# A two-layer encoder kernel: triangular inverses in halves of 16, conditioning tiles moved to the delta stage, a copy less in the attention norm, another order of the last rows

## The chip, the cores and the metric

The kernel runs on one core of one Trainium2 chip. The metric is device time in microseconds (us). The engines are PE (TensorE, matrix products; PEld is its weight load), DVE (VectorE), ACT (ScalarE), POOL (GpSimd) and SP (SyncE, which here only issues transfers). Each has a queue of its own that it works off in order; semaphores join them.

## The reference: what is computed

A (512, 1024) fp32 input passes two layers. Each has a token mixer (differential attention, pooling, a short convolution and a gated delta rule, four branches that are gated, summed and projected by `w_o`) and a channel mixer (a dense SwiGLU in layer 0, a top-2-of-8 mixture of experts in layer 1). Norms stand before and after each, and a conditioning vector `c` gives six scale, shift and gate vectors per layer through the weights `ada_w`. The parts that matter here:

```
oa = rms_norm(oa, diff_subln) * (1 - lambda_init)          # attention norm, per head
t_inv = triangular_solve(eye + m, eye, lower=True)         # m strictly lower, chunks of 64
u = t_inv @ (v * beta);  w = t_inv @ (k_beta * exp(g))
v_new = u_n - w_n @ state                                  # scan over chunks
o = qg_n @ state + attn_n @ v_new
state = state * exp(gl_n) + k_d.T @ v_new
```

## The kernel before, in words

An fp32 value is split into a high and a low part, and a product is three matmuls (lines 329 to 331, helper `mm3`). A weight chunk lands in one of three buffers named `raw`; ACT makes the high part (line 295), DVE the low part `wL` (line 296).

A layer's mixer first runs attention, then the delta rule: `delta_mats` (decay matrices, and the inverses), four `delta_group`s (two chunks each, a chain of small products and DVE steps), `delta_out`, and then the `w_o` stage with its norm. A *filler* (`set_fill`, `fill`) hands out PE work that depends on none of this (the merge projections `g_merge`, 128x512 products with weights `w_gb`), a few matmuls at a call, so that PE has work while a chain waits. A scheduler fixes the order on each engine when the program is built.

The inverse: 32 heads-by-chunk units are held as 32x32 diagonal blocks on four groups of 32 partitions. Line 740 negates the block into `Tb`, and the loop of lines 743 to 750 eliminates row after row: 30 steps of one multiply (746) and one subtract (748) on DVE, each up to 240 elements per partition, with a `fill` at every second step. Two transposes follow (752 into `Fi`, 753 into `F`), then copies of `F` and `Fi` into `KQ` (756 on ACT, 757 on DVE). `delta_group` begins with 32x32 products of `F` and `Fi` (793), and goes on through 801 (reads `KQ`), 833 (products with the state `S`), 835 (`vn`, DVE), 840 and 841 (outputs) and 846 (next state).

Conditioning: `g_ada` yields eight tiles for a vector. Each is a 512 KB load into a `raw` buffer (337, issued by SP) and a DVE reduction of 1.22 us (338). Vector (0,2) is a filler beside the merges from the start (`ADA_AT` 0); (0,4) and (0,3) are a filler of the `w_o` stage (argument `late` of `mixer`). In that stage line 380 sums squares with a product, 382 reads the sum on DVE, 384 takes the power on POOL and 390 spreads the factor with a product.

The attention norm (lines 1186 to 1204) does the like: 1191 sums, 1194 reads, 1196 takes the power into `ar`, 1199 copies `ar` over 64 columns into `bt` on DVE, 1201 multiplies `bt` with the identity (four 128x128 products, which the profile shows as eight), 1204 uses the result.

The end: `finish` adds the last expert's rows, norms them and scatters them to the output (2183 to 2194, an indirect transfer by POOL). Behind it stand two loops on a device value that is zero for this input, so that neither body is run: the first stores the last expert (`store`) and sums rows, the second handles windows (2317 and 2320).

Of the kernel before, what the change touches and what calls it, by code (L numbers as in the profile page):

```python
# [17 lines left out]
P = 128  # L18
T = 512
# [3 lines left out]
F = 2816  # L23
# [31 lines left out]
for _name, _w in [("c", KT), ("ada_b", NL * 6 * KT), ("mix_pre", NL * KT), ("mix_post", NL * KT),  # L55
# [16 lines left out]
FILL_ORD = "pbkzqsv"  # L72
ADA_AT = 0
ADA_E = 3
# [12 lines left out]

CST = [("ident", 128), ("ones", 128), ("tri", 128), ("neg", 128), ("edge", 32), ("bd2", 2), ("tok", 4), ("em8", 8),
       ("e8", 8)]
# [5 lines left out]
def shape_constants():  # L95
    c = np.zeros((P, NCST), np.float32), np.zeros((P, NMCST), np.float32)

    def put(name, a):
        late, o, w = C_AT[name]
        c[late][:, o:o + w] = a  # L100
# [18 lines left out]
    put("edge", edge.reshape(P, -1))  # L119
    put("bd2", np.stack([p < 64, p >= 64], 1))  # L120
    put("tok", p[:, None] + P * np.arange(4)[None])
    put("em8", np.tile(np.arange(8)[None] - 8, (P, 1)))
# [112 lines left out]
class Enc:  # L235
# [466 lines left out]
    def delta_mats(self, di):  # L702
# [32 lines left out]

        nc.vector.transpose(L, Sc.rearrange("p u j -> p j u"))
        R = dp.tile([P, 8, 2, 2, 64], FT, name="KQ").rearrange("p c a b t -> p (c a b) t")
        nc.gpsimd.memset(R, 0.0)
        Tb = di.tile([P, 32, 32], FT, name="Tb")
        nc.vector.tensor_scalar(Tb, L, -1.0, None, op0=OP.mult)  # L740
        nc.vector.memset(Tb.rearrange("p a b -> p (a b)")[:, 0:1024:33], 1.0)
        self.delta_prep(0)
        for j in range(1, 31):
            n = 31 - j
            t = di.tile([P, 256], FT, name="Tt", bufs=2)[:, :n * j].rearrange("p (a b) -> p a b", a=n)
            nc.vector.tensor_tensor(t, L[:, j + 1:, j:j + 1].to_broadcast([P, n, j]),
                                    Tb[:, j:j + 1, 0:j].to_broadcast([P, n, j]), op=OP.mult)
            nc.vector.tensor_tensor(Tb[:, j + 1:, 0:j], Tb[:, j + 1:, 0:j], t, op=OP.subtract)
            if j % FILL_T == 0:
                self.fill()  # L750
        dl["Ti"] = F, Fi = [dp.tile([P, 32, 32], FT, name=n) for n in ("F", "Fi")]
        nc.vector.transpose(Fi.rearrange("p u j -> p j u"), Tb)
        nc.vector.transpose(F.rearrange("p u j -> p j u"), Tb.rearrange("p a b -> p b a"))
        for q in range(4):
# [380 lines left out]
    def attention(self, l):  # L1135
# [6 lines left out]
        for pr in range(2):  # L1142
# [54 lines left out]
            pR = self.pt()  # L1197
            rb = self.tmp.tile([P, T], FT, name="bt", bufs=2).rearrange("p (a b c) -> p a b c", a=4, b=2)
            nc.vector.tensor_copy(rb, r.unsqueeze(3).to_broadcast([P, 4, 2, 64]))
            for b in range(4):  # L1200
                nc.tensor.matmul(pR[:, b * P:b * P + P], rb[:, b].rearrange("p a b -> p (a b)"), self.ident,
                                 start=True, stop=True)
            oo = self.tmp.tile([P, T], FT, name="bo", bufs=2)
# [31 lines left out]

    def mixer(self, l, ada, late, to):
        nc, tc = self.nc, self.tc
        self.lay = l
        with ExitStack() as es:
# [50 lines left out]
            self.post_begin(self.scale_col(l, 2, "mix_post", False))  # L1290
            self.set_fill(*[self.g_ada(*x) for x in late])
            for hv in range(2):
# [714 lines left out]

    def store(self, pool, e):

        nc = self.nc  # L2010
        for c, (s0, m, cp) in enumerate(self.blocks(e["cap"])):
            if not isinstance(e["po"][c], list):
                y = self.spare(3)
                nc.scalar.activation(y, e["po"][c], AF.Copy)
                for h in range(2):
                    nc.gpsimd.dma_start(self.yd[e["base"] + s0:e["base"] + s0 + m, h * T:h * T + T], y[64 * h:64 * h + m])
                continue
            for h in range(2):
                o, yh = e["po"][c][h], self.spare((0, 1, 3, 0)[2 * c + h])[:m]
                if cp == 2:  # L2020
                    t = self.bp.tile([P, T], FT, name="bo", bufs=2)
                    nc.scalar.activation(t[:m], o[m:2 * m], AF.Copy)
                    nc.vector.tensor_tensor(yh, o[:m], t[:m], op=OP.add)
                elif h == 0:
                    nc.scalar.activation(yh, o[:m], AF.Copy)
                else:
                    nc.vector.tensor_copy(yh, o[:m])
                nc.gpsimd.dma_start(self.yd[e["base"] + s0:e["base"] + s0 + m, h * T:h * T + T], yh)

# [147 lines left out]
    def finish(self, e):  # L2177

        nc = self.nc
        for c, (s0, m, cp) in enumerate(self.blocks(e["cap"])):  # L2180
            w, x, y = self.sw[:m, c, 1:2], self.sx[c][:m], self.sy[c]
# [7 lines left out]
            R = self.tm_rstd(y, EPS)  # L2189
            for h in range(2):  # L2190
                s = slice(h * T, h * T + T)
                nc.vector.scalar_tensor_tensor(y[h], y[h], R, self.G[:m, s], op0=OP.mult, op1=OP.mult)
                nc.vector.tensor_tensor(x[:, s], x[:, s], y[h], op=OP.add)
            nc.gpsimd.indirect_dma_start(out=self.out, out_offset=bass.IndirectOffsetOnAxis(ap=self.sid[:m, c, 0:1], axis=0),
                                         in_=x, in_offset=None)
# [42 lines left out]
    def moe(self):  # L2238
        nc, tc = self.nc, self.tc
        with ExitStack() as es:  # L2240
# [7 lines left out]
            with tc.tile_pool(name="mps", bufs=1, space=PS) as self.ps:  # L2248
# [66 lines left out]
                self.f = [self.bp.tile([P, T], FT, name=f"f{k}", bufs=1) for k in range(KT)]  # L2315
                n = nc.values_load(ints[0:1, 9 + NW:10 + NW], min_val=0, max_val=1)
                with tc.For_i(0, n):
                    self.store(mw, prev[0])
                    self.sum_rows(mw)
                with tc.For_i(0, n):  # L2320
                    it = mk.tile([P, 1], FT, name="kit")
# [44 lines left out]
    def run(self):  # L2366
# [15 lines left out]
        self.row_of(self.sc, sc)  # L2382
        self.mixer(0, [(0, 2)], [(0, 4), (0, 3)], None)
        self.ffn([(0, 5)] + [(1, v) for v in (1, 0, 2, 4, 3, 5)], self.xd, lambda: (self.scale_col(1, 1, "mix_pre", True), self.mod[1, 0]))
# [7 lines left out]
        nc.vector.tensor_copy(self.tokr, self.C("tok").unsqueeze(2).to_broadcast([P, 4, 2]))  # L2392
        self.mixer(1, [], [], None)
        es_st.close()
# [18 lines left out]
```

## Time and profile before

| | |
|---|---|
| median of three runs | 2619.18 us (2612.95 to 2620.56) |
| the profiled execution | 2621.02 us, of which the span is 2619.2 us |
| mean granted TensorE clock | 0.971 |
| PE busy | 2478.2 us (95%) |
| DVE, ACT, POOL busy | 1599.8 (61%), 1211.8 (46%), 304.1 us (12%) |
| DMA | 478.32 MB, mean 183 GB/s |

The span is the time from the first to the last instruction; the time has 1.8 us more around it. An engine that is busy 95% of the span sets the time, and a change helps where it shortens that engine's work or its idle stretches. A row of a timeline gives the start, the duration, the engine, the line, the operation, output and inputs, shape and count; in brackets stands how long the engine was idle before it, and what released it. A granted clock of 1.00 is 2.4 GHz, one of 0.50 is 1.2 GHz.

### The profile page before, as it was taken

Reading aid. Unit: us, or ns where it says so; the run is one execution under the profiler, and the core shown is the slowest. Engines: PE = TensorE matmul, PEld = TensorE weight load, DVE = VectorE, ACT = ScalarE, POOL = GpSimd, SP = SyncE. Lnnn points to the kernel's source line nnn. Section 1 sums busy time; section 2 is a strip of 40 time slices with the busy share of each in tenths; the row PEclk is TensorE's granted clock in tenths of the full one; section 3 lists DMA queues with packets and bytes.
Section 4 is the critical chain, followed back from the end, with each engine's and each line's share of the span. In section 5 each row is a group of like instructions: output and inputs, shape, how many; then the busy total and the mean of one; then the engine's idle time right before and its main releaser. Section 6 shows DMA issues by size and latency. Waiting matters only on the chain. (4 is left out here: it accounts for less than half of the span.)

```text
span 2619.2 us, 42410 instructions
## 1 busy us (share of the span) xinstructions
PE 2478.2 (95%) x16106; PEld 2012.9 (77%) x16106; DVE 1599.8 (61%) x2914; ACT 1211.8 (46%) x2153; POOL 304.1 (12%) x304
## 2 busy tenths in 40 slices
PE   7999899989999989999899979999999999999996
PEld 6667677889888888677678878886667767899885
DVE  7675833676545566675634556665555557866685
ACT  4554433443333354554333525554444446765574
POOL 0101222240000021103122110000000001000111
PEclk8999999999999999999999979999999999999998
DMA  7123122454565443121222338567889889975681
GB/s 266 57 69 127 61 72 72 152 176 165 179 211 202 144 147 105 49 77 46 77 71 73 111 120 326 210 224 286 309 304 351 324 306 347 383 272 209 239 320 64
DMA packets 124564, 478.32 MB, mean 183 GB/s; under 512 B 14224, under 2 KB 16912, under 8 KB 97600
## 3 DMA queue, kind: packets, MB, share of 16 engines
q1 hardware_dynamic: 119808, 460.19, 49.1%
q0 software_dynamic: 4544, 15.34, 1.7%
q8 instruction: 128, 2.10, 0.3%
q14 instruction: 84, 0.69, 0.1%
HBM read 462.17 MB, written 13.30 MB: 182 GB/s over the span
## 5 line engine op out<-in xcount | busy, mean ns | idle before, releaser
L329 PE MATMUL mm<-hH,wH 128*128 128x512 f32 (+1 forms) x1264 | 490.0, 389 | 9.0 <-ACT hH L1047 4.4
L331 PE MATMUL mm<-hH,wL 128*128 128x512 f32 (+1 forms) x1264 | 480.6, 380 | 5.0 <-DVE wL L296 4.8
L330 PE MATMUL mm<-hL,wH 128*128 128x512 f32 (+1 forms) x1264 | 480.2, 380 | 1.2 <-DVE hL L1282 1.1
L1847 DVE TENSOR_TENSOR mL<-mraw,mH 128x1024 fp32r<-128x1024 f32 x286 | 343.9, 1222 | 176.5 <-ACT mH L1846 121.1
L295 ACT ACTIVATE wH<-raw 128x512 fp32r<-128x512 f32 (+3 forms) x400 | 246.2, 624 | 419.2 <-PE mm L330 305.1
L296 DVE TENSOR_TENSOR wL<-raw,wH 128x512 fp32r<-128x512 f32 (+3 forms) x400 | 280.6, 716 | 214.0 <-ACT wH L295 212.5
L1846 ACT ACTIVATE mH<-mraw 128x1024 fp32r<-128x1024 f32 x286 | 297.6, 1054 | 151.7 <-PE gu L1870 48.5
L1869 PE MATMUL gu<-hH,mH 128*128 128x384 f32 (+1 forms) x1056 | 313.4, 365 | 2.3 <-DVE hL L1805 1.7
L329 PEld LDWEIGHTS mm<-hH,wH 128*128 128x128 f32 x1264 | 241.6, 191 | 63.0 <-issue 7.6
L331 PEld LDWEIGHTS mm<-hH,wL 128*128 128x128 f32 x1264 | 241.4, 191 | 56.3 <-DVE wL L296 8.4
L330 PEld LDWEIGHTS mm<-hL,wH 128*128 128x128 f32 x1264 | 242.4, 192 | 46.8 <-issue 5.9
L1870 PE MATMUL gu<-hH,mL 128*128 128x192 f32 (+1 forms) x1056 | 268.3, 254 | 0.0
L1869 PEld LDWEIGHTS gu<-hH,mH 128*128 128x128 f32 x1056 | 199.0, 188 | 15.1 <-issue 8.5
L1870 PEld LDWEIGHTS gu<-hH,mL 128*128 128x128 f32 x1056 | 202.3, 192 | 0.8
L1869 PE MATMUL gu<-hL,mH 128*128 128x384 f32 (+1 forms) x704 | 195.8, 356 | 0.0
L1847 DVE TENSOR_TENSOR mL<-f,mH 128x512 fp32r<-128x512 f32 x220 | 140.4, 685 | 74.1 <-ACT mH L1846 57.0
L1870 PE MATMUL gu<-hL,mL 128*128 128x192 f32 (+1 forms) x704 | 172.6, 245 | 0.0
L1846 ACT ACTIVATE mH<-f 128x512 fp32r<-128x512 f32 x220 | 126.4, 621 | 63.4 <-PE gu L1870 39.1
L1869 PEld LDWEIGHTS gu<-hL,mH 128*128 128x128 f32 x704 | 132.7, 189 | 9.1 <-issue 4.9
L1870 PEld LDWEIGHTS gu<-hL,mL 128*128 128x128 f32 x704 | 135.3, 192 | 1.5 <-issue 0.8
L338 DVE CUSTOM_DVE_ANT_0 adr<-adr,ada 128x1024 f32<-128x1024 f32 x56 | 68.6, 1224 | 103.3 <-DMA adr<-in_ada_w 103.3
L329 PE MATMUL mm<-mH,ma 128*128 128x512 f32 (+1 forms) x308 | 126.4, 410 | 0.4 <-ACT ma L1887 0.4
(643 smaller groups left out, 4397.6 us busy)
## 6 DMA issues: line engine op xcount, KB each, us to landing
mraw<-in_moe_w SPq DMA_DIRECT2D x209, 1024.0 KB
f<-in_moe_w SPq DMA_DIRECT2D x220, 256.0 KB
raw<-in_w_gb SPq DMA_DIRECT2D x64, 640.0 KB
adr<-in_ada_w SPq DMA_DIRECT2D x56, 512.0 KB
raw<-in_w_in SPq DMA_DIRECT2D x40, 512.0 KB
raw<-in_ada_w SPq DMA_DIRECT2D x32, 512.0 KB
raw<-in_ffn_d SPq DMA_DIRECT2D x58, 256.0 KB
raw<-in_ffn_g SPq DMA_DIRECT2D x24, 512.0 KB
```

The costliest lines, as they stand in the source:

```text
L295: self.nc.scalar.activation(h, part, AF.Copy)
L296: self.nc.vector.tensor_tensor(l, part, h, op=OP.subtract)
L329: t.matmul(out, W[0], X[0], start=start, stop=False)
L330: t.matmul(out, W[0], X[1], start=False, stop=False)
L331: self.last_mm = t.matmul(out, W[1], X[0], start=False, stop=stop).ins
L338: self.nc.vector.tensor_tensor_reduce(r, r, self.sc, 1.0, 0.0, op0=OP.mult, op1=OP.add, accum_out=t[:, m:m + 1])
L1846: self.mark(self.nc.scalar.activation(h[:, s], x, AF.Copy))
L1847: self.mark(self.nc.vector.tensor_tensor(l[:, s], x, h[:, s], op=OP.subtract))
L1869: t.matmul(pp[i][:, f, :2 * n], w[0], X[k][:, :, :n], start=k == 0, stop=False)
L1870: self.mark(t.matmul(pp[i][:, f, :n], w[1], X[k][:, 0, :n], start=False, stop=k == KT - 1))
```

## The change

Four edits. **Inverse:** the loop runs over two 16-row blocks at once (14 steps of four DVE operations, 14 to 56 elements), and the lower left quarter is had from PE: three blocks of 128 products of 32x32 (`blocks`, line 778 of the kernel after), two ACT copies, and four DVE subtractions from PSUM (791). POOL and ACT prepare two masked copies of the matrix. `F` is transposed first, `Fi` second. The loop has seven `fill`s where it had fifteen, and `blocks` has three.

**Conditioning tiles:** (0,4) and (0,3) become filler beside the merges together with (0,2), which now begins at merge step 60. All 24 tiles come behind the inverse of layer 0.

**Attention norm:** the copy 1199 is gone. The spreading product takes `ar` itself as a stationary operand that repeats one column 64 times, twice as many products with half the columns.

**Last rows:** `finish` multiplies by the norm's weights before the factor is known and has one operation less behind it; `store` of the last expert is moved ahead of the loops and always run, through SP; the two loops become one.

```diff
-ADA_AT = 0
+ADA_AT = 60
...
+            nc.gpsimd.memset(x[:, :, :16], 0.0)
+            nc.scalar.activation(x[:, :, 16:], Sc[:, 16 * i:16 * i + 16, 16:], AF.Copy, scale=self.C("lo16"))
+            So.append(x)
...
+        nc.gpsimd.memset(Tb[:, 16:, :16], 0.0)
         self.delta_prep(0)
-        for j in range(1, 31):
-            n = 31 - j
-            t = di.tile([P, 256], FT, name="Tt", bufs=2)[:, :n * j].rearrange("p (a b) -> p a b", a=n)
-            nc.vector.tensor_tensor(t, L[:, j + 1:, j:j + 1].to_broadcast([P, n, j]),
-                                    Tb[:, j:j + 1, 0:j].to_broadcast([P, n, j]), op=OP.mult)
-            nc.vector.tensor_tensor(Tb[:, j + 1:, 0:j], Tb[:, j + 1:, 0:j], t, op=OP.subtract)
+        for j in range(1, 15):
+            n = 15 - j
+            ts = []
+            for d in (0, 16):
+                t = di.tile([P, 64], FT, name="Tt", bufs=4)[:, :n * j].rearrange("p (a b) -> p a b", a=n)
+                nc.vector.tensor_tensor(t, L[:, d + j + 1:d + 16, d + j:d + j + 1].to_broadcast([P, n, j]),
+                                        Tb[:, d + j:d + j + 1, d:d + j].to_broadcast([P, n, j]), op=OP.mult)
+                ts.append(t)
+            for d, t in zip((0, 16), ts):
+                x = Tb[:, d + j + 1:d + 16, d:d + j]
+                nc.vector.tensor_tensor(x, x, t, op=OP.subtract)
             if j % FILL_T == 0:
                 self.fill()
...
+        def blocks(lhs, rhs, split=False):
...
+                        nc.tensor.matmul(p[r, u], x, rhs[r, 16 * i + u], start=True, stop=True,
+                                         tile_position=(32 * q, 32 * q))
+                out.append(p)
+            self.fill()
+            return out
...
+        for i, p in enumerate(blocks(So, F, True)):
+            nc.scalar.activation(Q[:, 16 * i:16 * i + 16], p, AF.Copy)
+        pa, pb = blocks(Q, Fi), blocks(Fi, Q)
+        for t, pp in ((Fi, pa), (F, pb)):
+            for i, p in enumerate(pp):
+                u = slice(16 * i, 16 * i + 16)
+                nc.vector.tensor_tensor(t[:, u], t[:, u], p, op=OP.subtract)
...
-            nc.vector.tensor_copy(rb, r.unsqueeze(3).to_broadcast([P, 4, 2, 64]))
             for b in range(4):
-                nc.tensor.matmul(pR[:, b * P:b * P + P], rb[:, b].rearrange("p a b -> p (a b)"), self.ident,
-                                 start=True, stop=True)
+                for hh in range(2):
+                    nc.tensor.matmul(pR[64 * hh:64 * hh + 64, b * P:b * P + P], r[:, b, hh:hh + 1].to_broadcast([P, 64]),
+                                     self.ident, start=True, stop=True)
...
-            self.set_fill(*[self.g_ada(*x) for x in late])
...
+            g = [self.spare(4 + 2 * c + h)[:m] for h in range(2)]
+            for h in range(2):
+                nc.vector.tensor_tensor(g[h], y[h], self.G[:m, h * T:h * T + T], op=OP.mult)
...
-                nc.vector.scalar_tensor_tensor(y[h], y[h], R, self.G[:m, s], op0=OP.mult, op1=OP.mult)
-                nc.vector.tensor_tensor(x[:, s], x[:, s], y[h], op=OP.add)
+                nc.vector.scalar_tensor_tensor(x[:, s], g[h], R, x[:, s], op0=OP.mult, op1=OP.add)
...
+                self.store(mw, prev[0], self.f)
                 with tc.For_i(0, n):
-                    self.store(mw, prev[0])
                     self.sum_rows(mw)
-                with tc.For_i(0, n):
...
-        self.mixer(0, [(0, 2)], [(0, 4), (0, 3)], None)
+        self.mixer(0, [(0, 2), (0, 4), (0, 3)], None)
```

How it moves instructions. On PE, before, layer 0: the last filler matmuls ahead of the first `delta_group` (line 793). `mm` is the accumulator of a merge, `hH`, `hL` the activations, `wH`, `wL` the weights.

```order
L329 MATMUL mm_3100<-hH5_87,wH_3092 128x512
L330 MATMUL mm_3100<-hL5_88,wH_3092 128x512
L331 MATMUL mm_3100<-hH5_87,wL_3093 128x512 [waits DVE_49]
L793 MATMUL pt_2915<-F_2899,Mt_2413 32x32 [waits DVE_49,PE_49]
L793 MATMUL pt_2915<-F_2899,Mt_2413 32x32
L793 MATMUL pt_2915<-Fi_2900,Mt_2413 32x32 x2
```

The same place after. Line numbers of the filler are one higher, 831 is the former 793, 986 a product of the pooling branch.

```order
L332 MATMUL mm_3074<-f2_1783,wL_2654 128x512
L330 MATMUL mm_3313<-hH0_77,wH_3295 128x512 [waits Activation_49]
L778 MATMUL pt_2799<-F_2794,Dm_2587 32x32 [waits DVE_49,PE_49]
L778 MATMUL pt_2799<-F_2794,Dm_2587 32x32 x63
...
L778 MATMUL pt_2940<-Fi_2795,Tb_2798 32x32 [waits Activation_49]
L778 MATMUL pt_2940<-Fi_2795,Tb_2798 32x32 x63
...
L778 MATMUL pt_3146<-Tb_2798,Fi_2795 32x32 [waits PE_49]
L778 MATMUL pt_3146<-Tb_2798,Fi_2795 32x32 x63
L986 MATMUL pt_3215<-x6_741,pw_3213 128x512 [waits DMAHW3_49,DVE_49]
L831 MATMUL pt_3239<-F_2794,Mt_2395 32x32 [waits DVE_49,PE_49]
```

The three blocks stand back to back: the fills between them were placed elsewhere. Behind the products of `delta_prep` (cst and qG), which stand alike in both, before has 161 of the 128x512 matmuls up to line 793, after has 67 up to the first line 778 (layer 1 the same). Between line 831 and the first product that reads `KQ` (839) stand two products of line 986 and some 14 filler matmuls.

On DVE, after, layer 0, behind the loop: 766 and 767 are the transposes, 297 is `wL`, 339 a conditioning tile, 1267 a merge step, 795 the copy into `KQ`.

```order
L766 STREAM_TRANSPOSE F_2794<-Tb_2595 128x32x32 [waits DVE_49,Pool_49]
L767 STREAM_TRANSPOSE Fi_2795<-Tb_2595 128x32x32
...
L297 TENSOR_TENSOR wL_3308<-raw_3303,wH_3307 128x640 [waits PE_49]
L339 ISA raw_3577,mod02_3576<-raw_3577,ada_122 128x1024 [waits DMAHW7_49,DVE_49]
...
L791 TENSOR_TENSOR Fi_2795<-Fi_2795,pt_2940 128x512 [waits PE_49]
L791 TENSOR_TENSOR F_2794<-F_2794,pt_3081 128x512
L339 ISA raw_3643,mod02_3576<-raw_3643,ada_122 128x1024 [waits DMAHW0_49,DVE_49]
...
L791 TENSOR_TENSOR Fi_2795<-Fi_2795,pt_3005 128x512 [waits PE_49]
L1267 SCALAR_TENSOR_TENSOR x6_3070<-th_2929,mm_2931 128x512 [waits PE_49]
L791 TENSOR_TENSOR F_2794<-F_2794,pt_3146 128x512
```

Before, the copies into `KQ` stood right behind the two transposes. Now two conditioning tiles stand among the subtractions: raw_3577 lies in the buffer that raw_3303 gives free, raw_3643 in the one that raw_3577 gives free. In layer 1 no conditioning tile stands there. The other 22 tiles follow one by one, up to the last group, most of them in a buffer that was freed one to seven DVE rows earlier. On SP the order of the loads there is:

```order
L277 DMA raw_3501<-in_w_gb 128x1280 [waits DMAHW3_49,DVE_49]
L338 DMA raw_3577<-in_ada_w 128x1024 [waits DMAHW4_49,DVE_49,Activation_49]
L338 DMA raw_3643<-in_ada_w 128x1024 [waits DVE_49]
L277 DMA raw_3682<-in_w_gb 128x1280 [waits DVE_49]
L277 DMA raw_3692<-in_w_gb 128x1280 [waits DMAHW5_49,DVE_49]
L338 DMA raw_3716<-in_ada_w 128x1024 [waits DMAHW6_49,DVE_49]
L338 DMA raw_3785<-in_ada_w 128x1024 [waits DVE_49]
```

Before, this stretch held loads of `w_gb` alone, and the 16 loads of (0,4) and (0,3) stood behind those of `w_o`.

## Rows read from the trace of the kernel before

**Rows 1.** The page, busy time, share of the span and instructions of each engine

```profile
PE 2478.2 (95%) x16106; PEld 2012.9 (77%) x16106; DVE 1599.8 (61%) x2914; ACT 1211.8 (46%) x2153; POOL 304.1 (12%) x304
```

**Rows 2.** Timeline of PE around the ends of the two inverses

```profile
306.34 0.50 PE L331 MATMUL mm<-hH,wL 128*128 128x512 f32 x1 [1.20 <-DVE wL L296]
326.64 0.26 PE L793 MATMUL pt<-F,Mt 32*32 32x32 f32 x2 [9.57 <-DVE F L753]
...
327.04 0.24 PE L793 MATMUL pt<-Fi,Mt 32*32 32x32 f32 x2
...
1279.62 0.26 PE L793 MATMUL pt<-F,Mt 32*32 32x32 f32 x2 [9.53 <-DVE F L753]
```

**Rows 3.** Stretches of 20 us: busy time of each engine, granted clock, DMA

```profile
240.00:260.00 20.00, 20.00 (x237) 15.02 (x236) 7.33 (x13) 8.35 (x14) 2.60 (x5) 1.00 0.42 144
320.00:340.00 20.00, 13.36 (x272) 10.66 (x273) 10.74 (x21) 9.45 (x21) 2.34 (x5) 0.74 0.22 68
540.00:560.00 20.00, 14.41 (x98) 14.00 (x98) 16.46 (x34) 6.66 (x18) 7.79 (x9) 0.83 0.64 211
```

**Rows 4.** Timeline of PE, filler products and a burst of sixteen 32x32 products

```profile
364.98 0.39 PE L329 MATMUL mm<-hH,wH 128*128 128x512 f32 x1
365.21 0.39 PE L330 MATMUL mm<-hL,wH 128*128 128x512 f32 x1
...
384.54 0.22 PE L793 MATMUL pt<-F,Mt 32*32 32x32 f32 x2
...
384.80 0.20 PE L793 MATMUL pt<-Fi,Mt 32*32 32x32 f32 x2
```

**Rows 5.** Timeline of DVE at the start and the end of the loop, layer 0

```profile
289.48 0.17 DVE L746 TENSOR_TENSOR Tt<-Fi,Tb 128x30 f32<-128x30 f32 x1
289.57 0.81 DVE L296 TENSOR_TENSOR wL<-raw,wH 128x640 fp32r<-128x640 f32 x1
290.31 0.21 DVE L748 TENSOR_TENSOR Tb<-Tb,Tt 128x30 f32<-128x30 f32 x1
290.55 0.22 DVE L746 TENSOR_TENSOR Tt<-Fi,Tb 128x58 f32<-128x58 f32 x1
...
324.54 1.95 DVE L753 STREAM_TRANSPOSE F<-Tb 128x1024 f32<-128x1024 f32 x1
326.59 1.75 DVE L757 COPY KQ<-F 32x512 f32<-32x512 f32 x4
```

**Rows 6.** Timeline of DVE, a conditioning tile and a merge step

```profile
248.47 1.23 DVE L338 CUSTOM_DVE_ANT_0 raw<-raw,ada 128x1024 f32<-128x1024 f32 x1 [3.39 <-DMA raw<-in_ada_w]
...
285.40 0.69 DVE L1230 SCALAR_TENSOR_TENSOR x<-th,mm 128x512 f32<-128x512 f32 x1
```

**Rows 7.** Timeline of PE in a delta group: products with the state, and with `vn`

```profile
362.87 0.68 PE L833 MATMUL pt<-S,wT 64*64 64x64 f32 x16
...
367.96 0.29 PE L841 MATMUL pt<-vn,At 64*64 64x64 f32 x4
```

**Rows 8.** Timelines of PE, DVE and POOL in the `w_o` stage of layer 0

```profile
540.99 0.60 PE L380 MATMUL pt<-cst,bt 128*128 128x1 f32 x4 [1.18 <-POOL bt L370]
545.34 1.23 DVE L338 CUSTOM_DVE_ANT_0 raw<-raw,ada 128x1024 f32<-128x1024 f32 x1 [0.68 <-DMA raw<-in_ada_w]
546.49 0.15 DVE L382 TENSOR_SCALAR rv<-pt 128x2 f32<-128x2 f32 x1
546.72 1.67 POOL L384 TENSOR_TENSOR rr<-rv,mhalf 128x2 f32<-128x2 f32 x1 [5.79 <-DVE rv L382]
548.45 1.22 PE L390 MATMUL pt<-cst,rr 128*128 128x128 f32 x4 [4.58 <-POOL rr L384]
```

**Rows 9.** Attention norm, the first of four: timelines of DVE and PE

```profile
141.10 0.43 DVE L1199 COPY bt<-ar 128x512 f32<-128x512 f32 x1 [1.77 <-POOL ar L1196]
141.58 1.16 PE L1201 MATMUL pt<-cst,bt 128*128 128x128 f32 x8 [1.40 <-DVE bt L1199]
```

**Rows 10.** The second loop at the end, POOL's queue: duration ns min/median/max, first and last start

```profile
L2320 POOLq EVENT_SEMAPHORE  x14: 17/43/43, 2611.2 to 2613.7; - x14
```

More of the change, by code (lines that the diff above doesn't have):

```diff
@@ L85 @@
 SUM_AT = 0
-CST = [("ident", 128), ("ones", 128), ("tri", 128), ("neg", 128), ("edge", 32), ("bd2", 2), ("tok", 4), ("em8", 8),
+CST = [("ident", 128), ("ones", 128), ("tri", 128), ("neg", 128), ("edge", 32), ("bd2", 2), ("lo16", 1), ("tok", 4), ("em8", 8),
        ("e8", 8)]
@@ L120, in shape_constants @@
     put("bd2", np.stack([p < 64, p >= 64], 1))
+    put("lo16", (p % 32 < 16)[:, None])
     put("tok", p[:, None] + P * np.arange(4)[None])
@@ L736, in delta_mats @@
         nc.vector.transpose(L, Sc.rearrange("p u j -> p j u"))
+        So = []
+        for i in range(2):
+            x = di.tile([P, 8, 64], FT, name="Dm", bufs=2).rearrange("p a b -> p (a b)").rearrange("p (u t) -> p u t", u=16)
+            nc.gpsimd.memset(x[:, :, :16], 0.0)
+            nc.scalar.activation(x[:, :, 16:], Sc[:, 16 * i:16 * i + 16, 16:], AF.Copy, scale=self.C("lo16"))
+            So.append(x)
         R = dp.tile([P, 8, 2, 2, 64], FT, name="KQ").rearrange("p c a b t -> p (c a b) t")
@@ L751, in delta_mats @@
         dl["Ti"] = F, Fi = [dp.tile([P, 32, 32], FT, name=n) for n in ("F", "Fi")]
+        nc.vector.transpose(F.rearrange("p u j -> p j u"), Tb.rearrange("p a b -> p b a"))
         nc.vector.transpose(Fi.rearrange("p u j -> p j u"), Tb)
-        nc.vector.transpose(F.rearrange("p u j -> p j u"), Tb.rearrange("p a b -> p b a"))
+        def blocks(lhs, rhs, split=False):
+            out = []
+            for i in range(2):
+                p = self.pt().rearrange("p (u t) -> p u t", u=16)
+                for u in range(16):
+                    for q in range(4):
+                        r = slice(32 * q, 32 * q + 32)
+                        x = lhs[i][r, u] if split else lhs[r, 16 * i + u]
+                        nc.tensor.matmul(p[r, u], x, rhs[r, 16 * i + u], start=True, stop=True,
[3 more added lines that the diff above has]
+            return out
+        Q = di.tile([P, 32, 32], FT, name="Tb")
+        for i, p in enumerate(blocks(So, F, True)):
[5 more added lines that the diff above has]
+                nc.vector.tensor_tensor(t[:, u], t[:, u], p, op=OP.subtract)
         for q in range(4):
@@ L1197, in attention @@
             pR = self.pt()
-            rb = self.tmp.tile([P, T], FT, name="bt", bufs=2).rearrange("p (a b c) -> p a b c", a=4, b=2)
-            nc.vector.tensor_copy(rb, r.unsqueeze(3).to_broadcast([P, 4, 2, 64]))
             for b in range(4):
-                nc.tensor.matmul(pR[:, b * P:b * P + P], rb[:, b].rearrange("p a b -> p (a b)"), self.ident,
-                                 start=True, stop=True)
+                for hh in range(2):
+                    nc.tensor.matmul(pR[64 * hh:64 * hh + 64, b * P:b * P + P], r[:, b, hh:hh + 1].to_broadcast([P, 64]),
+                                     self.ident, start=True, stop=True)
             oo = self.tmp.tile([P, T], FT, name="bo", bufs=2)
@@ L1234, in g_merge, with mixer @@
                     nc.gpsimd.tensor_tensor(self.mg[m], self.mg[m], t, op=OP.add)
-    def mixer(self, l, ada, late, to):
+    def mixer(self, l, ada, to):
         nc, tc = self.nc, self.tc
@@ L2006, in down_beside, with store @@
         return second
-    def store(self, pool, e):
+    def store(self, pool, e, room=None):
         nc = self.nc
+        room = room or [self.spare(k) for k in (0, 1, 3)]
+        queue = nc.gpsimd if len(room) == 3 else nc.sync
         for c, (s0, m, cp) in enumerate(self.blocks(e["cap"])):
             if not isinstance(e["po"][c], list):
-                y = self.spare(3)
+                y = room[2]
                 nc.scalar.activation(y, e["po"][c], AF.Copy)
@@ L2018, in store @@
             for h in range(2):
-                o, yh = e["po"][c][h], self.spare((0, 1, 3, 0)[2 * c + h])[:m]
+                o, yh = e["po"][c][h], room[(2 * c + h) % len(room)][:m]
                 if cp == 2:
@@ L2027, in store @@
                     nc.vector.tensor_copy(yh, o[:m])
-                nc.gpsimd.dma_start(self.yd[e["base"] + s0:e["base"] + s0 + m, h * T:h * T + T], yh)
+                queue.dma_start(self.yd[e["base"] + s0:e["base"] + s0 + m, h * T:h * T + T], yh)
     def g_places(self, R, mk, mp):
@@ L2179, in finish @@
         nc = self.nc
-        for c, (s0, m, cp) in enumerate(self.blocks(e["cap"])):
-            w, x, y = self.sw[:m, c, 1:2], self.sx[c][:m], self.sy[c]
+        bl = self.blocks(e["cap"])
+        done = []
+        for c, (s0, m, cp) in enumerate(bl):
+            w, y = self.sw[:m, c, 1:2], self.sy[c]
             for h in range(2):
@@ L2189, in finish @@
             R = self.tm_rstd(y, EPS)
+            g = [self.spare(4 + 2 * c + h)[:m] for h in range(2)]
+            for h in range(2):
+                nc.vector.tensor_tensor(g[h], y[h], self.G[:m, h * T:h * T + T], op=OP.mult)
+            done.append((R, g))
+        for c, (s0, m, cp) in enumerate(bl):
+            x, (R, g) = self.sx[c][:m], done[c]
             for h in range(2):
                 s = slice(h * T, h * T + T)
-                nc.vector.scalar_tensor_tensor(y[h], y[h], R, self.G[:m, s], op0=OP.mult, op1=OP.mult)
-                nc.vector.tensor_tensor(x[:, s], x[:, s], y[h], op=OP.add)
+                nc.vector.scalar_tensor_tensor(x[:, s], g[h], R, x[:, s], op0=OP.mult, op1=OP.add)
             nc.gpsimd.indirect_dma_start(out=self.out, out_offset=bass.IndirectOffsetOnAxis(ap=self.sid[:m, c, 0:1], axis=0),
@@ L2392, in run @@
         nc.vector.tensor_copy(self.tokr, self.C("tok").unsqueeze(2).to_broadcast([P, 4, 2]))
-        self.mixer(1, [], [], None)
+        self.mixer(1, [], None)
         es_st.close()
```

## Prediction

> **What bounds the kernel now.** I read the page first: PE is busy 95% of the span [rows 1], so a stretch shortens only where PE waits, runs at the low clock, or has less to do. The idle time of DVE, ACT and POOL costs nothing unless PE waits at its end. Next I read the timeline of PE for its waits near the edited lines. At each inverse PE waits about 9.5 us for the transpose into `F`, after about 1.2 us for a `wL` [rows 2] (of layer 1 the rows hold the long wait; the short one I take to be like that of layer 0). Then the clock in stretches of 20 us: 0.74 around the inverse of layer 0 and 0.83 around the norm of the `w_o` stage [rows 3]. With two levels, 1.00 and 0.50, a mean of 0.74 is 20 x 0.26 / 0.5 = 10.4 us at the low one, and 0.83 is 6.8 us. The idle stretches in them were 9.57 and 4.58 us [rows 2, 8], so either way some 5 us (an estimate, the half that is not idle) lie behind the end of the wait. Work of 5 us at half rate loses 2.5 us.
>
> **Inverse, what goes.** Per layer the wait of 9.5, that of 1.2 and the clock's 2.5: 13.2 us.
>
> **Inverse, what comes.** First, PE has 94 filler matmuls less ahead of it. That work isn't saved: the merges are handed out later, in a stretch where PE has no idle time to take it up. At 0.23 us each [rows 4] it is 21.6 us. Before, PE stopped at 326.64 - 9.57 = 317.07 [rows 2], 1.2 us of it a wait, so now it reaches the first 32x32 product at 317.07 - 1.2 - 21.6 = 294.3.
>
> When is `F` there? The loop began at 289.48; the `wL` that ran among its first operations now stands ahead of it, so 290.3 [rows 5]. A dependent operation starts 0.24 us after one of 0.21 [rows 5]; operations of 14 to 56 elements are nearer to the 30-element one, 0.17 to 0.21, so I take 0.225 from link to link. A step is two links, with the other block's pair between them if two independent operations overlap: the rows show a subtraction starting 0.07 us before an independent 0.81 us operation has ended [rows 5]. Then 14 x 0.45 = 6.3 us. Bounds: 6.3 and, if nothing overlaps, 56 x 0.225 = 12.6. I take 6.3. Two `wL` in the loop add 1.5, the transpose 1.95 [rows 5], its release 0.15: `F` at 300.2. PE is idle for 5.9 us.
>
> Sixteen products of 32x32 on four groups of partitions start within 0.26 us at the full clock [rows 4], 0.40 behind the idle stretch [rows 2]: 0.017 and 0.027 us each. A block of 128 takes 2.2 or 3.4 us, three take 6.6 to 10.2. With 5 us at the low clock (187 products) and 197 at the full one: 8.4. The ACT copies of the first half run beside the second half. Sum 5.9 + 8.4 = 14.3, against 13.2: a loss of 1.1 us per layer. **The inverse is ready 18 us sooner, but PE gains nothing, because its wait is half as long and the products fill the other half.**
>
> On whether small products are that cheap, the row says 0.017 us for a product of two matmuls. The Trainium skill ("TensorEngine Tiling (Array Packing)", section Performance Considerations) says that each matmul carries about 60 cycles of overhead however few columns it has; by that 768 matmuls at 25 ns would take 19.2 us instead of 8.4, an estimate from that page. Sixteen products in 0.26 us are 8 ns a matmul, so the row speaks against it for a burst, and no row shows a run of 256.
>
> **Layer 0 alone: the tiles among the subtractions.** DVE comes from `Fi` at 301.9, does two activation splits (0.6 each) and a `wL`, and frees raw_3303 at 303.9. Only then can raw_3577 load, and a load takes 3.4 us to land: the tile at 248.47 waited 3.39 us behind the one that freed its buffer [rows 6]. The reduction is 1.23 [rows 6], so 308.5. The subtractions of `Fi` and `F`, a 128x512 read from PSUM as the merge step of 0.69 [rows 6], end at 309.9. The second tile loads into the buffer just freed: 308.5 + 3.4 + 1.23 = 313.1; then two subtractions with a merge step between, 315.2, another operation, 315.8, the `KQ` copies of 1.75 [rows 5], 317.6. PE ends the blocks at 300.2 + 8.4 = 308.6, has one 986 product (four passes of 0.23, estimated at 0.9), waits 0.4 for `F`, then has 0.3 of line 831, 0.9 and 14 x 0.23 = 3.2 of filler, and stands at line 839 at 314.3. It waits 3.3 there. Together 3.7 us. Queued behind the tile on DVE are these subtractions, and behind them all of the first delta group. Bounds: 0 if the loads land sooner, 7 if they take 1.5 us more each. Layer 1 has no tile there: its copies end some 4 us behind the blocks, and PE has 4.9 us of work till then.
>
> **Conditioning tiles, what goes.** In the `w_o` stage the sum of line 380 was done at 541.6, but DVE read it (382) only at 546.49, behind reductions that waited for loads; POOL took 1.67, and PE waited 4.58 [rows 8]. Without them: 541.6 + 0.2 + 1.7 = 543.5, and PE runs out of filler at 548.45 - 4.58 = 543.9. The wait goes whole, and the clock's 2.4: 7.0 us. Late next is the 1.18 wait ahead of line 380 for POOL's squares, which stays. Bounds 4.6 (the clock falls anyway) and 8.2 (that wait goes too).
>
> **What comes.** 22 tiles more in the delta groups. A DVE step there has from 363.5 to 367.96, 4.4 us, between its input and PE's need [rows 7]; a tile whose load starts right ahead of it holds the queue for 3.4 + 1.23 = 4.6, and the step itself takes 0.4: late by 0.6 to 0.7. Three of the 22 stand one or two rows behind the release of their buffer: 2 us. Bounds: 0, since PE was busy 20.00 of 20 us in the stretch that held the 3.39 wait [rows 3, 6], and 15 (all 22 late).
>
> **Attention norm.** The copy of 0.43 is on the path, PE waits for it [rows 9]: 4 norms, -1.7 us. The product takes 1.16 for its eight [rows 9]; sixteen of half the columns cost the same if the halves run side by side, up to 1.1 more if not: bounds -1.7 and +2.7.
>
> **Last rows.** One loop less: the second spans 2611.2 to 2613.7 on POOL's queue [rows 10], -2.5. The factor's last operation is shorter, but the second block's work and the copies of `store` now stand ahead on DVE: I count 0. The four stores land while POOL's scatter does. Bounds -4.5 and 0.
>
> **The sum.** 2 x 1.1 + 3.7 - 7.0 + 2.0 - 1.7 - 2.5 = -3.3 us against the profiled execution's 2621.0. The median of the runs is 1.8 below that, 2619.2, so I expect 2615.9. 0.3% is 7.9 us, about what a measurement of this kernel can tell from no change: under 2611.3 is faster, over 2627.1 slower.
>
> **Rivals.** (a) *DVE's pairs don't overlap*: the loop takes 12.6, PE waits 6.3 longer twice, +9.3 against before: 2628. For it: each operation waits for a semaphore. Against it: the overlap in [rows 5].
> (b) *The other side: the tiles hold DVE.* Each of the 22 stands in a buffer freed shortly before, and SP's later loads queue behind. If each makes the step behind it 0.7 late, 15.4 in place of 2.0: +10, 2629. It decides from some 18 late tiles on. For it: 3.4 + 1.23 is over the 4.4 of a step. Against it: the 20.00 of [rows 3].
> (c) *Small products have a floor.* At the pace of the 64x64 products, 16 in 0.68 us [rows 7], of which some 0.2 is the length of the last one (that of one in [rows 4]), a matmul takes 0.029 us: 768 take 22 us, not 8.4, +27 over the sum: 2643. This is where the page above points.
> (d) *More is won.* The clock doesn't fall in a wait of 5.9 (idle 5.9 and blocks 6.6, -0.7 per layer), the loads land in time (no 3.7, no 2.0) and the 1.18 wait goes: -1.4 - 8.2 - 1.7 - 2.5 = -13.8: 2605. For it: DMA is under half busy in these stretches [rows 3].
>
> **Chances.** The forecast (2610 to 2622) 0.42, (a) 0.11, (b) 0.13, (c) 0.06, (d) 0.24, else 0.04. Faster is (d), a sixth of the forecast's and a part of the rest: 0.33. Slower is (b), (c) and half of (a): 0.24. Same: 0.43. The range that leaves out (c) and the ends: 2604 to 2630.
>
> **What would show it.** On PE, line 778 should begin near 300 on a wait of about 6 us for `F`, and three blocks take 7 to 10 us in both layers; in layer 0 alone waits for DVE's subtractions follow. The wait ahead of line 390 should be gone, the norm's waits 0.4 shorter, the end 2.5 shorter. I am wrong if the delta groups show PE waits for DVE of over 5 us in all, if the wait for `F` is over 10 or nothing, or if the displaced filler finds idle time that I don't see.

## The result, and the profile after

The changed kernel takes 2659.6 us (median of 4 runs, 2656.3 to 2661.7), the kernel before 2619.9 beside it: a ratio of 1.0156, 95% interval 1.0140 to 1.0172, that is 39.7 us more. It is slower, and outside the predicted range. The profiled execution has a span of 2656.5 us.

First the page, to compare with [rows 1]: busy time, share and instructions of each engine, and the queue that brings instructions (packets, MB, share of 16 engines).

```profile
PE 2504.3 (94%) x17674; PEld 2031.4 (76%) x17674; DVE 1583.2 (60%) x2913; ACT 1215.8 (46%) x2164; POOL 304.6 (11%) x310
...
q8 instruction: 140, 2.29, 0.3%
```

PE has 1568 matmuls and as many weight loads more, but only 26 us more of busy time, so a good part of the 39.7 us must be idle or slow time. A 32x32 product of the kernel's text stands in the trace as two matmuls, so the 384 products of the three blocks of a layer are 768 matmuls; from here on the matmuls are counted. The same queue had 128 packets in the kernel before:

```profile
q8 instruction: 128, 2.10, 0.3%
```

That is 12 more for 3136 instructions, 261 each. The timeline of PE at the inverse of layer 0 answers to [rows 2].

```profile
300.12 2.20 PE L778 MATMUL pt<-F,Dm 32*32 32x32 f32 x147 [7.27 <-DVE F L766]
303.39 1.65 PE L778 MATMUL pt<-F,Dm 32*32 32x32 f32 x107 [1.07 <-issue]
...
307.39 1.93 PE L778 MATMUL pt<-Fi,Tb 32*32 32x32 f32 x128 [2.08 <-issue]
311.12 1.65 PE L778 MATMUL pt<-Fi,Tb 32*32 32x32 f32 x107 [1.80 <-issue]
...
314.58 1.93 PE L778 MATMUL pt<-Tb,Fi 32*32 32x32 f32 x128 [1.53 <-issue]
318.03 1.71 PE L778 MATMUL pt<-Tb,Fi 32*32 32x32 f32 x109 [1.53 <-issue]
319.67 1.22 PE L986 MATMUL pt<-x,pw 128*128 128x512 f32 x1
```

The blocks begin at 300.1, as predicted, but they end at 319.67, not at 308.6. They come in portions: 147 matmuls first, then 128 at a time in 1.9 us (the rows of 107 are 128 with the 21 that the "..." leaves out, the first of the next block). Behind each portion PE stands for 1.1 to 2.1 us although nothing that the profile shows is awaited ("issue"; in layer 1 up to 3.2 us). The stops fall inside the blocks, and the borders between blocks are crossed without one. A portion begins every 3.3 to 4.0 us. Stretches of 20 us, to compare with [rows 3]:

```profile
300.00:320.00 20.00, 11.88 (x769) 11.22 (x770) 7.47 (x11) 1.19 (x2) 0.00 (x0) 0.50 0.22 61
...
1270.00:1290.00 20.00, 10.07 (x668) 9.43 (x668) 5.51 (x7) 1.19 (x2) 0.00 (x0) 0.50 0.13 37
...
555.00:575.00 20.00, 18.45 (x153) 18.11 (x153) 8.24 (x18) 6.84 (x20) 10.01 (x14) 1.00 0.01 2
```

In the first two, the inverses, PE is busy for 10 to 12 of the 20 us, and the granted clock is 0.50, the lower level, throughout. The third is the `w_o` stage. The view of the DMA queues tells what else happens there: the instruction packets in the blocks of layer 0 (300.12 to 319.67), then in a stretch of filler (262 to 288).

```profile
q8 instruction: 6, 0.10, 2.1%
...
q8 instruction: 1, 0.02, 0.2%
```

Six packets bring the 1536 instructions of the three blocks (768 matmuls, each with its weight load), 256 each, and 128 matmuls with their loads are one such portion. Cut into shorter stretches, the view has one packet in each of 301.0 to 302.5, 304.2 to 306.0, 308.2 to 310.0, 312.0 to 314.0, 315.3 to 317.0 and 319.0 to 320.6: one to every portion of PE.

The trace has the start and the length of each packet, and the stops follow them. In layer 0 packets have landed at 302.11, 305.97, 309.66, 313.19 and 316.49 us, and PE goes on at 303.39, 307.39, 311.12, 314.58 and 318.03, each time 1.3 to 1.5 us later. In layer 1 it is 1.2 to 1.4 us at all five stops, which last 1.2 to 3.2 us: where PE stands longest, the packet came latest.

A second wait is new, at the norm of the delta branch (the products of line 923 take the normed `dO`; the merge steps are lines 1270 and 1271):

```profile
471.31 0.69 DVE L1270 SCALAR_TENSOR_TENSOR bt<-th,mm 128x512 f32<-128x512 f32 x1
471.92 0.82 DVE L297 TENSOR_TENSOR wL<-raw,wH 128x640 fp32r<-128x640 f32 x1
472.65 1.26 DVE L911 TENSOR_SCALAR ssO<-ssO 128x16 f32<-128x16 f32 x1
...
472.08 1.80 POOL L1271 TENSOR_TENSOR x<-x,bt 128x512 f32<-128x512 f32 x1 [0.80 <-DVE bt L1270]
473.99 2.91 POOL L913 TENSOR_TENSOR rO<-ssO,mhalf 128x16 f32<-128x16 f32 x1
...
478.31 1.13 PE L923 MATMUL pt<-cst,dO 128*128 128x128 f32 x8 [3.86 <-DVE dO L914]
```

Before, the same product (line 885) stood without a wait, and POOL had been idle for 5 us ahead of the factor (line 875):

```profile
460.36 2.91 POOL L875 TENSOR_TENSOR rO<-ssO,mhalf 128x16 f32<-128x16 f32 x1 [4.93 <-DVE ssO L873]
...
464.84 1.39 PE L885 MATMUL pt<-cst,dO 128*128 128x128 f32 x11
```

Now merge steps stand between the sum and the factor on DVE and POOL, and PE has only the same 36 filler matmuls (8.2 us) to cover a chain that grew from 8.5 to 12.5 us (from the start of the last product of line 841, now 879, to that of line 885, now 923).

In the `w_o` stage the edit did what it should. Compared with [rows 8] (lines one higher) the waits of 1.18 and 4.58 us are gone, and the clock around them is 1.00 (the third stretch above) in place of 0.83 [rows 3]. The second sum begins 12.78 us behind the first (560.90 to 573.68); before, the two were 20.86 apart (540.99 to the last row here, which is of the kernel before).

```profile
560.90 0.60 PE L381 MATMUL pt<-cst,bt 128*128 128x1 f32 x4
...
563.61 0.61 PE L391 MATMUL pt<-cst,rr 128*128 128x128 f32 x4
...
573.68 0.61 PE L381 MATMUL pt<-cst,bt 128*128 128x1 f32 x4 [1.55 <-POOL bt L371]
...
561.85 0.61 PE L380 MATMUL pt<-cst,bt 128*128 128x1 f32 x4 [1.86 <-POOL bt L370]
```

DVE around the end of the loop and the subtractions, to compare with [rows 5]:

```profile
297.43 0.25 DVE L757 TENSOR_TENSOR Tt<-Fi,Tb 128x14 f32<-128x14 f32 x2
...
297.99 1.98 DVE L766 STREAM_TRANSPOSE F<-Tb 128x1024 f32<-128x1024 f32 x1
...
308.22 1.23 DVE L339 CUSTOM_DVE_ANT_0 raw<-raw,ada 128x1024 f32<-128x1024 f32 x1 [4.64 <-DMA raw<-in_ada_w]
...
316.33 0.69 DVE L791 TENSOR_TENSOR Fi<-Fi,pt 128x512 f32<-128x512 f32 x1 [6.87 <-PE pt L778]
```

The two multiplies of a pair of blocks together take 0.25 us, so the pairs overlap, and the loop ends on the predicted time. The conditioning tile waits 4.64 us for its load, but afterwards DVE itself waits 6.87 us for PE: the tile is hidden behind the long blocks.

### The profile page after: what moved, and what is told of

It is laid out like the page before. It is cut to its first block, busy times and chain, and to the rows that moved or that the text cites. A ratio compares the mean times of both kernels' runs of the same rounds, so it can differ in the third digit from the quotient of the medians.

```text
span 2656.5 us, 45481 instructions
## 1 busy us (share of the span) xinstructions
PE 2504.3 (94%) x17674; PEld 2031.4 (76%) x17674; DVE 1583.2 (60%) x2913; ACT 1215.8 (46%) x2164; POOL 304.6 (11%) x310
```

## Experiments

The question is why the blocks take 19.5 us. My theory from the portions: PE's instructions come too slowly for a long run of small products (the expectations call this the supply theory). Its rivals: the array's time, a fixed price of every small product, and a loss that lies in another part of the change. Each edit is against the changed kernel, or for `e5` to `e9` and `e12` against the kernel before. Ratios are to the kernel before on the same chip.

**The inverse undone** (`e1_inverse_undone`: the change with `delta_mats` as it was).

> The changed kernel with the inverse of before (30 steps on DVE, no 32x32 products of line 778); the other three edits stay. If the inverse is the whole loss (theory), the rest gives what its stages showed in the trace after: the wait ahead of the spreading product of the w_o stage gone with its clock, -7.7 us, the end -2.1, the attention norm 0: 2610 us (2605 to 2615), and PE's waits at the transposes are 9.5 us again. If the conditioning tiles in the delta stage are what costs (rival b), it stays over 2635.

Measured: 2613.6 us, ratio 0.9970 [0.9956, 0.9985]. Without the new inverse the change is a gain of 8.6 us, as expected (2605 to 2615), and the waits at the transposes are 8.9 and 9.5 us. The loss lies in the inverse.

**Twice the columns** (`e2_wide_products`).

> Each of the 768 products of line 778 (per layer 384 products, two matmuls each) takes 64 moving columns where it took 32 (a neighbour's too, so the inverse is wrong): twice the array work, the same number of instructions. Theory of supply (PE gets its instructions in portions of 128 weight loads and 128 matmuls, one in 3.3 to 4 us, and runs dry between): the stretch of line 778 stays at 19 to 21 us per layer, the total within 4 us of the changed kernel. Rival, the clock (array time at 1.2 GHz is what costs): the stretch grows to 28 us or more per layer, the total by 16 us or more.

```diff
-                        nc.tensor.matmul(p[r, u], x, rhs[r, 16 * i + u], start=True, stop=True,
+                        v = u // 2 * 2
+                        nc.tensor.matmul(p[r, v:v + 2], x, rhs[r, 16 * i + v:16 * i + v + 2], start=True, stop=True,
```

Measured: 2661.1 us, 1.0154 [1.0132, 1.0177], the time of the changed kernel (the number of matmuls is the same too, 17674, so other values did not change the loops behind). The blocks, line 779 here, and the waits of PE from 285 to 325 us (us in total, times, longest):

```profile
297.35 6.11 PE L779 MATMUL pt<-F,Dm 32*32 32x64 f32 x256 [7.34 <-DVE F L766]
...
304.58 1.99 PE L779 MATMUL pt<-Fi,Tb 32*32 32x64 f32 x128 [0.81 <-issue]
```

```profile
PE pt L779 <- DVE F L766: 7.3, 1, 7.3
PE pt L779 <- issue: 6.0, 4, 2.8
```

The blocks take 21.5 us (297.35 to 318.82) in place of 19.55, a little over the 19 to 21 expected. Twice the array work fills some of the idle time: "issue" falls from 8.0 to 6.0. The clock did not stay at 0.50, as the rival's 28 us assumed: between 297.35 and 318.82 it is 0.81, so the time alone does not decide. But PE still stands for 6 us, and at 24 ns a matmul the first 256 run without a stop, where the changed kernel stops behind 147. So the array's time is not the limit.

**Filler between the half blocks** (`e3_spread`; `e4_spread_more` is the same with `FILL_T = 1`, which hands out more filler in the loop).

> The changed kernel with two fills (12 filler matmuls, 2.7 us) placed behind each half block of 64 products, by an order edge on PE alone. Supply theory: during the filler the next portion arrives, so the waits inside line 778 go and the products cost 7 to 9 us per layer instead of 19.5: 11 us less per layer, about 2637 us (2630 to 2644). Rival, a floor of 25 ns for a small matmul: 64 products still take 3.2 us, the sum of the products' time stays near 19 us, the total stays over 2652.

> As the spread kernel, and a fill at each of the 14 steps of the loop instead of at every second. Supply theory: the wait of 7 us for F is filled too (7 fills of 1.36 us) and the clock stays high, so that the inverse costs less than the 13 us that it cost before: 2612 us (2604 to 2622), under the kernel before. Floor rival: over 2635.

```diff
-FILL_T = 2
+FILL_T = 1
...
+                with self.tc.issue_after(self.last_mm):
...
+                            last = nc.tensor.matmul(p[r, u], x, rhs[r, 16 * i + u], start=True, stop=True,
...
+                with self.tc.issue_after(last.ins):
+                    self.fill(2)
```

Measured: `e3` 2651.6 us, 1.0117 [1.0096, 1.0138]; `e4` 2639.0 us, 1.0067 [1.0046, 1.0087]. The timeline of PE in `e4` (rows of filler left out), and in the end its waits from 280 to 480 us:

```profile
297.99 1.93 PE L779 MATMUL pt<-F,Dm 32*32 32x32 f32 x128 [4.39 <-DVE F L766]
...
304.30 1.29 PE L779 MATMUL pt<-F,Dm 32*32 32x32 f32 x128
...
308.46 1.29 PE L779 MATMUL pt<-Fi,Tb 32*32 32x32 f32 x128
...
321.94 1.29 PE L779 MATMUL pt<-Tb,Fi 32*32 32x32 f32 x128
```

```profile
PE pt L925 <- DVE dO L916: 7.2, 1, 7.2
PE pt L779 <- DVE F L766: 4.4, 1, 4.4
...
PE pt L779 <- issue: 0.5, 2, 0.3
```

With 4.2 to 6.3 us from one portion of 128 to the next the "issue" waits fall from 8.0 to 0.5 us, the clock of 300 to 320 rises from 0.50 to 0.92, and a portion takes 1.29 us, 10 ns a matmul. Without the stops all six take 8.4 us in layer 0 and 8.5 in layer 1, the predicted price. But the filler that stands there is missing later: none of the 36 filler matmuls is left at the delta branch's norm, and the wait there grows from 3.9 to 7.2 us.

By their totals both runs missed the supply theory's ranges: `e4` lies in the floor rival's, `e3` just under it. What speaks against the floor is the trace, not the total. In `e3` the matmuls take 8.2 us without their stops, as expected, but stops of 2.8 us a layer remain, and the wait for `F` grows to 10.2, since the filler between the half blocks is taken from ahead of it.

**The parts alone**, each put into the kernel before (`e5` the inverse, `e6` the tiles, `e7` the norm, `e8` the last rows), by the hunks of the diff shown ahead of the prediction.

> The kernel before with the new inverse and nothing else. Theory (the inverse is the whole loss, and the two layers cost it alike): about 47 us slower than before, since the changed kernel is 40 slower and its other edits won about 8: 2667 us (2660 to 2673). Rival: the loss comes from the meeting of the inverse with the conditioning tiles on DVE, then the inverse alone costs under 35 us, and layer 0 is the better for it.

> The kernel before with all 24 conditioning tiles beside the merges from step 60, nothing else. Theory: the w_o stage's wait of 4.6 us and its clock go, the tiles cost PE nothing in the delta groups: 7 us faster, ratio 0.997 (0.9955 to 0.999). Rival b of the prediction: over 1.000.

> The kernel before with the attention norm's copy taken away, nothing else. As predicted, -1.7 us (ratio 0.9993). By the trace after: PE's wait ahead of the spreading product is as long as before (1.41 where 1.40 stood), since the scheduler puts one or two filler matmuls less ahead of it: 0 (ratio 0.9985 to 1.0015), and the four waits are 1.2 to 1.5 us each.

> The kernel before with the last rows rearranged, nothing else. -2.1 us from the trace after (26.9 us from the last filler matmul's start to the end of the span before, 24.8 after), ratio 0.9992 (0.998 to 1.0005). Rival: 0, the loop's end hides in the scatter of the output.

| part | us | ratio, interval | against before, us |
|---|---|---|---|
| inverse | 2666.5 | 1.0164 [1.0140, 1.0189] | +43.8 |
| tiles | 2610.3 | 0.9952 [0.9934, 0.9969] | -12.4 |
| norm | 2627.2 | 1.0019 [1.0005, 1.0032] | +4.5 |
| last rows | 2618.6 | 0.9978 [0.9965, 0.9992] | -4.1 |

The sum is +31.8 against +39.7 measured together; the interval of each is 3.5 to 6.5 us to either side, so they agree. The inverse came out as expected. Tiles and last rows gained slightly more than their ranges held (0.9952 against 0.9955, 0.9978 against 0.998), and the norm lost where nothing was expected (1.0019, range up to 1.0015). The waits of PE in layer 0 of `e5` (280 to 480 us) show that both new waits come from the inverse alone:

```profile
PE pt L778 <- issue: 9.5, 5, 3.4
PE pt L778 <- DVE F L766: 7.3, 1, 7.3
PE pt L923 <- DVE dO L914: 4.2, 1, 4.2
```

PE's waits between 1000 and 1185 us show why the norm gains nothing, in `e7` and then before:

```profile
PE pt L1200 <- POOL ar L1196: 3.1, 2, 1.8
...
PE pt L1201 <- DVE bt L1199: 2.6, 2, 1.3
```

Before, the copy ended two waits of 2.6 us together in this stretch; now POOL's `ar` ends two of 3.1. From the last attention product (line 1183) to the first of line 698 in layer 1 the kernels with this edit (the changed one, `e1`, `e7`) take 5.03, 4.96 and 4.93 us longer than before, those without it (`e5`, `e6`, `e8`, `e9`) 0.07 or less. In `e7` 19 merge matmuls (4.4 us) more stand there, and as many fewer in the 170 us ahead, which gets no shorter. Why they are handed out later wasn't tried.

**Tiles and last rows together** (`e9_tiles_and_end`, the kernel before with these two parts of the diff).

> The kernel before with the two edits that won alone (conditioning tiles, last rows), without the new inverse and the norm's edit. If they add up: -12.4 and -4.1 us by their own runs, ratio 0.994 (0.992 to 0.996), the fastest of all kernels here. If the profile's waits alone count (6.1 and 2.3 us in the w_o stage with the clock behind them, 2.0 at the end), ratio 0.996.

Measured: 2608.3 us, 0.9948 [0.9931, 0.9965], faster than the kernel before and the changed one, and not told apart from the tiles alone (2610.3). Together the parts gain 14.6 us, as they add up.

**Less filler between the portions** (`e10_spread_less`: `e4` with `self.fill(1)` and the norm's copy put back).

> The changed kernel without the norm's edit, a fill at each of the 14 steps and one fill (6 filler matmuls, 1.4 us) behind each half block, where the second spread kernel had two. Filler is a stock: that kernel used it up, so that PE waited 7.4 us for the norm of the delta branch in each layer. Six fills fewer leave 8.2 us for that place: its wait goes back under 3 us, while 64 products and one fill, 2.6 us, are shorter than a portion's 3.3 us, which gives back 3 to 5 us per layer inside line 779. Sum: 2632 us (2624 to 2640). If filler is not what is missing there, the wait stays at 7 us.

Measured: 2639.6 us, 1.0059 [1.0041, 1.0077], at the upper end of the range and no better than `e4`. The stops cost some 4 us a layer, as expected, and the wait for `F` is 4.4. But the wait at the delta branch's norm is still 6.8 us (7.2 in `e4`), not under 3: only 6 filler matmuls stand there (none in `e4`, 36 in the changed kernel), so the filler saved between the portions did not come to that place. The run does not test whether it would have helped.

**One block in place of three** (`e11_one_block`).

> The changed kernel with the first of the three blocks alone: the second and third are left out, their results replaced by the first's (so the inverse is wrong); the four subtractions stay, as do the fills. Supply theory: a third of the products, 6.5 us in place of 19.5 per layer, -26 us: 2634 us (2628 to 2642). Rival, the products cost what the burst's row says (8.4 us) and the rest of the loss is elsewhere: -11 us, 2649.

```diff
-        pa, pb = blocks(Q, Fi), blocks(Fi, Q)
-        for t, pp in ((Fi, pa), (F, pb)):
-            for i, p in enumerate(pp):
+        for t in (Fi, F):
+            for i in range(2):
...
-                nc.vector.tensor_tensor(t[:, u], t[:, u], p, op=OP.subtract)
+                nc.vector.tensor_tensor(t[:, u], t[:, u], Q[:, u], op=OP.subtract)
+        self.fill(2)
```

Measured: 2959.0 us, 1.1282. The total can't be read: other values choose other experts, and the loops over them run differently (PE has 17558 matmuls, where 16650 would be left). Up to there the trace can be read against that of the changed kernel. PE at the one block of layer 0:

```profile
298.77 2.20 PE L778 MATMUL pt<-F,Dm 32*32 32x32 f32 x147 [7.31 <-DVE F L766]
302.44 1.71 PE L778 MATMUL pt<-F,Dm 32*32 32x32 f32 x109 [1.47 <-issue]
304.08 2.08 PE L986 MATMUL pt<-x,pw 128*128 128x512 f32 x2
```

From the first product to the row of line 986 the block takes 5.3 us, in layer 1 4.9 (1253.25 to 1258.11), 14.2 and 16.1 us less than the three blocks. That is 30.3 us in two layers, nearer to the supply theory's 26 than to the rival's 11. A block thus costs some 5 us if it is the first and 7 to 8 if it follows another, in place of the predicted 2.2 to 3.4.

**The kernel before with less filler** (`e12_fewer_fills`: `FILL_T = 4`).

> The kernel before, its loop with a fill at every fourth step, nothing else: about 47 filler matmuls less ahead of the end of the inverse. If displaced filler is not absorbed later, PE waits 10.7 us longer for the transpose in each layer and the total is 21 us longer or a little more (ratio 1.0085, 1.007 to 1.011). If the delta groups and the norm behind them take it up, under 8 us (ratio under 1.003).

Measured: 2634.1 us, 1.0045 [1.0023, 1.0066], 11.1 us more, between the two forecasts. PE's wait at the end of the inverse:

```profile
322.27 0.27 PE L793 MATMUL pt<-F,Mt 32*32 32x32 f32 x2 [16.93 <-DVE F L753]
```

It grows by 7.4 us per layer, less than expected, because the loop too ends 4.4 us sooner, without the filler's operations on DVE. Of 14.8 us of longer wait in two layers 11.1 come back as time (interval 6 to 17): most of the filler taken out ahead of a wait is lost.

## Why the prediction was wrong

**The step that failed** is "three take 6.6 to 10.2", the price of the products. It was taken from a burst of sixteen [rows 4], and the runs here are of 768 matmuls. The pace within a portion was nearly right (15 ns a matmul at the lower clock, 10 at the full one in `e4`; the prediction had 13 and 8). What failed is that the pace can be held: after each 256 instructions PE stands. In place of 8.4 the blocks take 19.5 us in layer 0 and 20.9 in layer 1 (1270.74 to 1291.66). The sign named for it, blocks of 7 to 10 us, failed in both layers. The difference is 23.6 us, over half of the 43.0 by which the sum missed (-3.3 predicted, +39.7 measured).

Shown: the limit isn't the array (`e2`: twice the columns in 21.5 us, with 6 us of stops left), nor a fixed price of each matmul (`e4`: 10 ns), nor a wait for data (the stops fall inside a block whose operands are in use already, 128 matmuls apart). That it is the supply of instructions rests on the portions of 128 matmuls with 128 loads, on one instruction packet for each of them, on the pace that is free again in `e4`, and on the time of the packets. In the changed kernel, `e2`, `e3`, `e5`, `e10` and `e11` PE has 37 stops of 0.5 to 3.5 us inside the blocks, and each ends 1.2 to 1.6 us after an instruction packet has landed. No run supplied the same stream faster, and what sets the time of a packet stays open. The Trainium skill ("Runtime: NRT & Kernel Launch", section Instruction fetch mechanics) says that instructions come in blocks of 16 KiB, 256 instructions, the next fetched while the current one runs, and calls the cost of crossing mostly hidden. The first half agrees with the six packets for 1536 instructions; the second doesn't where 256 instructions run in 1.9 us: 1.1 to 2.1 us show at each crossing in layer 0.

**Rival (c)** had the direction but not the mechanism. Its 22 us for the blocks are close to the measured 19.5, but by a price of each matmul, which `e4` excludes. So are the 19.2 us estimated from the Trainium skill ("TensorEngine Tiling (Array Packing)", section Performance Considerations). The agreement in size is chance.

**The second miss** is the delta branch's norm, 3.9 us a layer. The prediction had the displaced filler take its time where "PE has no idle time to take it up"; it did so, but it also brought its merge steps on DVE and POOL into a chain that filler had just covered. `e5` has the wait, `e1` and `e6`, with the old inverse, don't. In `e4` and `e10`, where little or no filler is left at that place, it is 6.8 to 7.2.

**The inverse, the other terms.** The wait for `F` was 7.3, predicted 5.9; the blocks began at 300.12, predicted 300.2; pairs overlap, so rival (a) is out. That the filler isn't saved holds: `e12`. In layer 0 the waits and the blocks are now 7.3 + 19.5 + 3.9 = 30.7 us, in layer 1 32.1, against 9.5 + 1.2 each before: +41.4 in all; `e5` measured +43.8.

**Tiles.** The `w_o` stage gained as told (predicted -7.0, bounds 4.6 and 8.2; from the first sum to the second the changed kernel takes 20.86 - 12.78 = 8.1 us less, and the wait of 1.18 ahead of the first sum, which was to stay, is gone too). The 3.7 us in layer 0 and the 2.0 in the delta groups didn't come: the first is hidden behind the blocks, and PE's waits from 280 to 480 us in the changed kernel ("issue", `F` and `dO`) and in `e6` name no step of a delta group. So rival (b) is out, and the part alone gives -12.4 [-17.3, -8.1] where -5.0 was reckoned (-7.0 and 2.0; the 3.7 needs the new inverse). Where the tiles gain more than the `w_o` stage shows isn't located.

**Norm.** Predicted -1.7, measured +4.5 [+1.3, +8.4]: the copy went, and the wait stayed with POOL's `ar` as what is late next: at the first norm it is 1.41 us in the changed kernel, 1.40 before [rows 9]. **Last rows.** Predicted -2.5; from the last expert matmul (line 1977, now 2013) to the end the trace has 23.3 us in place of 25.5, 2.2 less, and the part alone gives -4.1 [-9.2, -2.1].

**Would the inverse pay if its instructions came in time?** In `e4` they nearly do, and per layer PE still spends 4.4 on `F`, 0.5 on "issue", 8.4 on the products and 7.2 at the norm: 20.5 us, against 10.7 of waits before. It doesn't, as long as the filler that hides the blocks is taken from the place behind them.

## What to carry to other kernels

Price a long run of small matmuls by its count of instructions as well as by its columns, and take the price from a run as long as the planned one: here 256 instructions in 1.9 us outran what came after, while the same portions 4.2 us and more apart ran almost freely. Filler is a stock: spent ahead of one wait it is missing at the next, and its own steps on other engines go where it goes. Measure the parts of a change apart: two of the four gain 14.6 us together, and the other two had hidden that.

## What was not expected of the hardware

In 20 us of 32x32 matmuls with stops of 1.1 to 3.2 us the granted clock stays at 0.50 throughout, although PE is busy for 10 to 12 of the 20 us. With twice the columns (`e2`) it is 0.81 over the blocks of layer 0, and with filler of 128x512 between the portions (`e4`) 0.92 from 300 to 320 us and 1.00 from 1270 to 1290.

Matmuls of 32x32 on four groups of partitions run at 10 ns each in portions of 128 at the full clock, weight loads included. The Trainium skill ("TensorEngine Tiling (Array Packing)", section Performance Considerations) gives each matmul about 60 cycles of overhead, 25 ns at 2.4 GHz by estimate; these portions and the burst of [rows 4] lie below it.

PE goes on 1.2 to 1.6 us after an instruction packet has landed, at every stop inside the blocks that these runs show. And even a filler matmul behind such a portion can stand for instructions: in `e3` one does for 1.87 us, and it too goes on 1.4 us after a packet.
